# A hybrid encoder trunk on one core: the inverse root's division placed beside ScalarE's root, first rows scaled out of PSUM, two gates moved to VectorE, and a layer norm cut into token tiles

## The chip, the cores and the metric

The kernel runs on one core of one Trainium2 chip. The metric is the device time of one execution in microseconds (us); the median of three runs stands for a kernel.

## The reference

The input `x` has 256 tokens of 2048 features (float32). Two layers follow each other; each is a token mixer and a squared-ReLU MLP (2048 to 8192 to 2048), each with an RMS norm ahead of it and a residual add behind it, and a last RMS norm closes the trunk. The first layer's mixer is the one that the change touches:

```python
def conv_module(h, w_pw1, b_pw1, w_dw, b_dw, ln_g, ln_b, w_pw2, b_pw2):
    u = h @ w_pw1 + b_pw1
    a, gate = jnp.split(u, 2, axis=-1)
    u = a * jax.nn.sigmoid(gate)
    u = lax.conv_general_dilated(...) + b_dw   # causal, depthwise, 31 taps
    u = jax.nn.silu(layer_norm(u, ln_g, ln_b))
    return u @ w_pw2 + b_pw2
```

Here `h` is `x * rsqrt(mean(x*x) + 1e-6) * g`. The second layer's mixer is latent attention, which the change leaves alone but for the inverse roots of its norms.

## The kernel before, in words

All matrix products are made of two float32r parts of each operand, an upper part (`hi`, a copy by ScalarE in `upper_half`, L163) and a lower part (`lo`, the rest, subtracted by VectorE or GpSimd in `lower_half`, L167), in three products. Weights come in pieces of 0.5 to 1 MB on SyncE's queue into three buffers (`load`, L146 to L155). Inside `tc.manual_schedule()` every engine takes its instructions in the order of the program text, so the text is the schedule. TensorE has filler in that schedule: transposes of the identity that nobody reads (`busy` L748, L796, `keep_warm` L233), with counts in `N_WARM`, `N_WARM_GAP` and `N_WARM_LN`.

**The start (L510 to L833).** ScalarE's queue issues the 16 KB of norm gains (`stage_rows`, L514) and then the second 128 tokens of `x`; SyncE's queue issues the first 128 tokens, each in three pieces (L515 to L518). The gains are transposed (L735) and copied to `vecs` (L736). TensorE transposes `x` into PSUM (`turn0`, L762), 8 blocks of 128 columns for each token tile, then 4 more. VectorE takes the mean squares of the first token tile with `bn_stats` (L746), ScalarE those of the second with `Square` (L744). L776 to L784 bring them to `r0`, the inverse root (`rsqrt`, L213 to L226: ScalarE's `Sqrt` L218, then four dependent VectorE steps L222 to L225). TensorE spreads `r0` into a row of PSUM (L787), VectorE copies the row to SBUF (L791), and then scales the transposed blocks in place by gain and row (`scaled`, L798 to L803), block 0 first. ScalarE makes their upper parts (`upper`, L814), VectorE the lower ones (`lower`, L817), and the first products of the convolution's first matrix follow (`conv_mm`, L556 to L569).

**The chunks (L866 to L910).** The 16 chunks of 128 features go by in turn: products of chunk c on TensorE, while chunk c-1 gets its gate (`glu`, L580: a sigmoid on ScalarE, then either one VectorE operation, L588, or a bias on ScalarE, L593, and a product on GpSimd, L594) and its 31 taps. Of the taps, ScalarE starts two sums in PSUM (`start_sum`, L624), VectorE adds most of them (`add_tap`, L653, in an order found by `dve_taps`, L676), ScalarE makes some products apart (`product`, L599) and GpSimd adds those up (`side_sum`, L646). For the last chunk, 15 taps are products with diagonal matrices on TensorE (`last_products`, L617), 7 are added by VectorE, and 8 products are summed by GpSimd.

**The layer norm (L911 to L998).** Each chunk is transposed to tokens (`to_tokens`, L708) for its statistics (`ln_stats`, L719 to L723; the last pair of chunks together by `bn_stats`, L723). `bn_aggr` (L919) gives mean and variance, TensorE spreads them (L926), VectorE subtracts the mean and multiplies by the inverse root (`ln_op`, L930 to L933), ScalarE applies `Silu` (L947), VectorE makes the lower part (L957), and the products of the second matrix follow (L993). Ahead of each new function on ScalarE, `warm` (L228) issues a dummy activation, so that the table is loaded there.

**The end (L1543 to L1582).** `finish` has its own copy of the inverse root (L1556 to L1561), scales the rows and stores them.

## Time and profile before

| what | value |
|---|---|
| median of 3 runs | 1976.75 us (1976.64 to 1977.14) |
| the profiled execution, its own time | 1976.61 us |
| the span of its trace | 1974.8 us |
| TensorE busy | 1959.7 us, 99% |
| VectorE, ScalarE, GpSimd busy | 1265.8, 989.0, 221.4 us |
| moved by DMA | 367.58 MB, mean 186 GB/s |

Times in the rows of a profile are microseconds from the span's start; a timeline row has start, duration (or the stretch that merged instructions fill), engine, line, operation, output and input, count, and in brackets how long the engine had been idle before it and what ended that. PE is TensorE's products, PEld its loads of the stationary operand, DVE is VectorE, ACT ScalarE, POOL GpSimd, SPq and ACTq the queues that issue DMAs. The filler transposes count as busy time of PE, and the ends of products are modelled, so the 99% alone doesn't say that the products set the time.

### The profile page before, as it was taken

The page shows a single profiled execution, that of the slowest core. Times are in us where ns is not written, and L with a number is a line of the kernel's source. Part 1 is how long each engine was busy: PE and PEld are TensorE (multiplying, and loading weights), DVE is VectorE, ACT ScalarE, POOL GpSimd, SP SyncE. Part 2 cuts the span into 40 slices and gives each one's busy share as a digit, 9 for nine tenths or more (in the row PEclk, how much of TensorE's full clock was granted, in tenths as well). Part 3 has the DMA queues.
Part 4 walks back from the last instruction along what each step waited for, and adds up shares of the span by engine and source line. Part 5 has one row for each costly group of instructions (what it writes and reads, how often), then busy time and mean ns, then how long its engine had stood idle before and what let it go on. Part 6 is the DMA issues. An engine that isn't in the chain of part 4 may idle for free.

```text
span 1974.8 us, 27819 instructions
## 1 busy us (share of the span) xinstructions
PE 1959.7 (99%) x10981; PEld 1718.3 (87%) x10981; DVE 1265.8 (64%) x1914; ACT 989.0 (50%) x1427; POOL 221.4 (11%) x183
## 2 busy tenths in 40 slices
PE   9999999999999999999999999999999999999998
PEld 8999888888888888888899998888888888888886
DVE  7999987755444556666656666866555445665554
ACT  5667755544333445444456655554443334544443
POOL 6999100000000000000002310000000000000000
PEclk9999999999999999999999999999999999999999
DMA  7766456665555666556554445666655566665553
GB/s 232 208 187 181 168 182 205 189 190 190 193 196 194 190 188 191 191 191 194 186 186 140 139 150 171 209 196 192 192 192 192 192 191 192 192 192 192 192 192 107
DMA packets 243875, 367.58 MB, mean 186 GB/s; under 512 B 15512, under 2 KB 90528, under 8 KB 243488
## 3 DMA queue, kind: packets, MB, share of 16 engines
q1 hardware_dynamic: 242416, 363.28, 57.9%
q10 hardware_dynamic: 1328, 2.52, 0.4%
q8 instruction: 86, 1.41, 0.3%
q14 instruction: 45, 0.37, 0.0%
HBM read 363.68 MB, written 2.10 MB: 185 GB/s over the span
## 4 chain that ended last, share of the span: by engine, by line
PE 97%; ACT 1%; DVE 1%; DMA 0%; POOL 0%; issue 0%; ACTq 0%; DVEq 0%
PE acc L465 23%; PE acc L198 15%; PE acc L196 15%; PE acc L197 15%; PE acc L466 12%; PE acc L566 9%; PE acc L993 2%; DMA xs<-in_x 0%; PE acc L1380 0%; PE tr L254 0%; ACT hi L163 0%; PE acc L1244 0%; PE acc L1246 0%; PE acc L1245 0%; DVE lo L167 0%; PE tr L1371 0%
## 5 line engine op out<-in xcount | busy, mean ns | idle before, releaser
L167 DVE TENSOR_TENSOR lo<-raw,hi 128x1024 fp32r<-128x1024 f32 (+1 forms) x631 | 760.6, 1211 | 635.3 <-ACT hi L163 630.1
L163 ACT ACTIVATE hi<-raw 128x1024 fp32r<-128x1024 f32 (+1 forms) x696 | 723.3, 1047 | 756.2 <-PE acc L197 427.5
L465 PE MATMUL acc<-xt,hi 128*128 128x512 f32 x2048 | 710.3, 390 | 0.0
L466 PE MATMUL acc<-xt,lo 128*128 128x256 f32 x2048 | 577.5, 282 | 0.0
L465 PEld LDWEIGHTS acc<-xt,hi 128*128 128x128 f32 x2048 | 384.4, 188 | 80.7
L197 PE MATMUL acc<-hi,gl 128*128 128x512 f32 (+1 forms) x1028 | 399.1, 388 | 0.0
L198 PE MATMUL acc<-lo,gh 128*128 128x512 f32 (+1 forms) x1028 | 399.1, 388 | 0.0
L196 PE MATMUL acc<-hi,gh 128*128 128x512 f32 (+1 forms) x1028 | 399.1, 388 | 0.0
L466 PEld LDWEIGHTS acc<-xt,lo 128*128 128x128 f32 x2048 | 387.1, 189 | 0.2
L198 PEld LDWEIGHTS acc<-lo,gh 128*128 128x128 f32 x1028 | 193.0, 188 | 39.8
L197 PEld LDWEIGHTS acc<-hi,gl 128*128 128x128 f32 x1028 | 193.0, 188 | 39.7
L196 PEld LDWEIGHTS acc<-hi,gh 128*128 128x128 f32 x1028 | 193.0, 188 | 39.7
L566 PE MATMUL acc<-xt,hi 128*128 128x256 f32 x1024 | 180.0, 281 | 0.3 <-ACT xt L814 0.2
L653 DVE SCALAR_TENSOR_TENSOR sum<-ub,w_dw,sum 128x256 f32<-128x256 f32 x410 | 164.8, 486 | 4.2 <-ACT sum L624 3.8
L167 POOL TENSOR_TENSOR lo<-raw,hi 128x1024 fp32r<-128x1024 f32 x65 | 155.0, 2409 | 14.8 <-ACT hi L163 14.8
L566 PEld LDWEIGHTS acc<-xt,hi 128*128 128x128 f32 x1024 | 154.6, 188 | 1.1 <-ACT xt L814 0.7
L566 PE MATMUL acc<-xt,lo 128*128 128x256 f32 x512 | 139.2, 279 | 0.0
L566 PEld LDWEIGHTS acc<-xt,lo 128*128 128x128 f32 x512 | 94.6, 188 | 0.0
L1175 POOL MEMSET pad_kv<- 128x8 f32 x1 | 0.1, 105 | 770.7 <-DVE xt L209 770.7
L477 ACT ACTIVATE v<-acc 128x256 f32<-128x256 f32 x128 | 46.3, 382 | 24.9 <-PE acc L466 24.9
L196 PE MATMUL acc<-hi,oh 128*128 128x512 f32 x128 | 50.6, 395 | 0.0
L198 PE MATMUL acc<-lo,oh 128*128 128x512 f32 x128 | 50.0, 391 | 0.0
(272 smaller groups left out, 1724.3 us busy)
## 6 DMA issues: line engine op xcount, KB each, us to landing
raw<-in_mlp_w SPq DMA_DIRECT2D x256, 1024.0 KB, 5.1
raw<-in_conv_w_pw SPq DMA_DIRECT2D x62, 512.0 KB, 5.1
raw<-in_conv_w_pw SPq DMA_DIRECT2D x16, 1024.0 KB, 5.0
raw<-in_mla_w_o SPq DMA_DIRECT2D x16, 1024.0 KB, 5.6
raw<-in_mla_w_kv_up SPq DMA_DIRECT2D x8, 1024.0 KB, 5.6
raw<-in_mla_w_in SPq DMA_DIRECT2D x8, 576.0 KB, 3.7
raw<-in_mla_w_in SPq DMA_DIRECT2D x4, 1024.0 KB
raw<-in_mla_w_q_up SPq DMA_DIRECT2D x16, 256.0 KB, 3.1
```

The lines of the kernel that those rows point to most:

```text
L163: nc.scalar.activation(hi, raw[:, js, :], AF.Copy)
L167: eng.tensor_tensor(lo, raw, hi.bitcast(F32), op=ALU.subtract)
L196: nc.tensor.matmul(ps, sh, mh, start=start, stop=False)
L197: nc.tensor.matmul(ps, sl, mh, start=False, stop=False)
L198: nc.tensor.matmul(ps, sh, ml, start=False, stop=stop)
L465: nc.tensor.matmul(ps[b], wh[:, bs], xhl(k), start=k == 0, stop=False)
L466: nc.tensor.matmul(ps[b][:, :S], wl[:, bs], xh(k), start=False, stop=k == KC - 1)
L477: nc.scalar.activation(v[:, b, :], o[:, S:], AF.Copy)
L566: nc.tensor.matmul(pss[c][b][:, :S], w[i][:, bs], (xh, xl)[j](k), start=k == i + j == 0, stop=end and k == k0 + nk - 1 and (i, j) == terms ...
L653: nc.vector.scalar_tensor_tensor(out=out, in0=ubs[c][:, w : w + S], scalar=tap(c, w), in1=base, op0=ALU.mult, op1=ALU.add)
L993: nc.tensor.matmul(ps2[b][t], x_kt(k, t), w[:, bs], start=k == g == i == 0, stop=k == KC - 1 and i == len(group) - 1,)
L1175: nc.gpsimd.memset(pad_kv, 0.0)
```

## The change

1. **Inverse root.** `rsqrt` and `finish` share `refined`: with `s` the root and `v` the mean square, it divides 1 by `v` (not by `s`), multiplies by `s`, and makes the same Newton step from there. The division needs no root. It is four VectorE operations as before.
2. **Start.** The gains' 16 KB are issued behind `x` on ScalarE's queue; their transposition and copy move from the head of TensorE's and VectorE's order to behind all of `x`'s transpositions; VectorE's copy now stands ahead of L776. Two new VectorE copies (`early`) bring blocks 0 and 1 to SBUF ahead of the last `bn_stats`; `scaled` for these two reads them and takes the spread row straight from PSUM. The row's copy to SBUF goes to ScalarE, behind the first `hi`. The dummy sigmoid moves from there to the end of the first chunk, and half a weight split (the second half of piece 3) moves behind the first gate.
3. **Gates.** The zero margins of the three gate buffers are set once, at the start, on GpSimd. Chunk 14's gate is one VectorE operation, as that of chunks 0 and 15 was.
4. **Last chunk.** Two more taps of chunk 14 go first on VectorE; the last sum of chunk 15 (L882) is cut in two token tiles; the last two chunks have their statistics taken apart (four `bn_stats` of 128 columns, not two of 256) from three PSUM tiles, not one.
5. **Layer norm.** Multiplication by the inverse root and the first `Silu` of block 0 go by token tiles, and the first products take token tile 0 first.
6. **Filler and room.** 6 for 12 transposes ahead of the first products, 1, 9, 4, 6 for 3, 12, 6, 9 around the layer norm; `PAD_SMALL` 48 for 16, and the gate buffers lie in another pool, so that tiles behind them in SBUF lie elsewhere.

```diff
-PAD_SMALL = 16
+PAD_SMALL = 48
-N_WARM = (5, 0, 16, 12)
+N_WARM = (5, 0, 16, 6)
-N_WARM_LN = (3, 12, 6, 9)
+N_WARM_LN = (1, 9, 4, 6)
...
+    def refined(s, v, y, t):
+        nc.vector.reciprocal(t, v)
+        nc.vector.tensor_tensor(y, s, t, op=ALU.mult)
+        nc.vector.scalar_tensor_tensor(out=t, in0=y, scalar=-0.5, in1=s, op0=ALU.mult, op1=ALU.mult)
+        nc.vector.scalar_tensor_tensor(out=y, in0=t, scalar=1.5, in1=y, op0=ALU.add, op1=ALU.mult)
...
-        nc.scalar.activation(t, ms, AF.Sqrt, bias=eps_cols[eps])
+        nc.scalar.activation(r, ms, AF.Sqrt, bias=eps_cols[eps])
         nc.vector.tensor_scalar(v, ms, scalar1=eps, scalar2=None, op0=ALU.add)
-        nc.vector.reciprocal(y, t)
-        nc.vector.scalar_tensor_tensor(out=t, in0=y, scalar=-0.5, in1=y, op0=ALU.mult, op1=ALU.mult)
-        nc.vector.tensor_tensor(t, t, v, op=ALU.mult)
-        nc.vector.scalar_tensor_tensor(out=y, in0=t, scalar=1.5, in1=y, op0=ALU.add, op1=ALU.mult)
+        refined(r, v, y, t)
...
-        vecs_rows = stage_rows(cv, vec_rows, nc.scalar)
         for i in range(3):
             for t in range(T):
                 c0, c1 = X_PARTS[t][i]
                 (nc.sync, nc.scalar)[t].dma_start(xs[:, t, c0:c1], x[0, t * P : (t + 1) * P, c0:c1])
+        vecs_rows = stage_rows(cv, vec_rows, nc.scalar)
...
+        branches = [cv.tile([P, PAD + S], F32, name=nm("ub")) for _ in range(3)]
+        for ub in branches:
+            nc.gpsimd.memset(ub[:, 0:PAD], 0.0)
...
-            ub = ubs[c] = cv2.tile([P, PAD + S], F32, tag="ub", name=nm("ub"), bufs=3)
-            (nc.vector if c in (0, KC - 1) else nc.gpsimd).memset(ub[:, 0:PAD], 0.0)
+            ub = ubs[c] = branches[c % 3]
...
-            if c in (0, KC - 1):
+            if c in (0, KC - 2, KC - 1):
...
-            turn(n_vecs, vecs_rows, misc)
-            nc.vector.tensor_copy(vecs[:, :n_vecs], misc[:, :n_vecs])
...
-            for n in range(NNB):
+            def squares(n):
                 nc.vector.bn_stats(xst[:, n, :], xs[:, 0, n * NB : (n + 1) * NB])
+            for n in range(NNB - 1):
+                squares(n)
...
+            early = [xn[:, 0, (i + 1) * S : (i + 2) * S] for i in range(2)]
+            for i in range(2):
+                nc.vector.tensor_copy(early[i], where[i])
+            squares(NNB - 1)
             for t in range(T):
                 turn0(range(8, 12), t)
+            pss[0] = [acc_tile()]
+            turn(n_vecs, vecs_rows, pss[0][0])
+            nc.vector.tensor_copy(vecs[:, :n_vecs], pss[0][0][:, :n_vecs])
             busy(N_WARM[2])
...
-            nc.vector.tensor_copy(r_row, misc[:, :S])
             conv_half(0, 0)
-            warm(AF.Sigmoid)
-            pss[0] = [acc_tile() for _ in range(2)]
+            nc.scalar.activation(r_row, misc[:, :S], AF.Copy)
+            pss[0].append(acc_tile())
...
-                        out=where[k], in0=where[k], scalar=g_mix[0][:, k : k + 1], in1=r_row,
+                        out=where[k], in0=early[k] if k < 2 else where[k], scalar=g_mix[0][:, k : k + 1],
+                        in1=misc[:, :S] if k < 2 else r_row,
...
-                    conv_split(3)
+                    warm(AF.Sigmoid)
+                    conv_half(3, 0)
...
+                    for _ in range(2):
+                        dve_step(KC - 2, 0)
                     dve_taps(KC - 1)
...
-                    nc.vector.tensor_tensor(ca[:, c, :], last_sum[0], halves[c], op=ALU.add)
+                    for t in range(T):
+                        ts = slice(t * P, (t + 1) * P)
+                        nc.vector.tensor_tensor(ca[:, c, ts], last_sum[0][:, ts], halves[c][:, ts], op=ALU.add)
...
-                if c > 1:
+                if c == 1:
+                    conv_half(n + 1, 1)
+                else:
...
             to_tokens(KC - 1)
+            ln_stats(KC - 2)
             ln_stats(KC - 1)
...
-                    swish(sh[:, k, :], k)
+                    for t in range(T if k == 0 else 1):
+                        swish(sh, k, slice(t * P, (t + 1) * P) if k == 0 else slice(0, S))
...
-            ln_op(0, 1, scale, ALU.mult)
+            for t in range(T):
+                ln_op(0, 1, scale, ALU.mult, t)
...
+                        order = [(b, t) for b in range(2) for t in range(T)]
+                        if k == 0:
+                            order.sort(key=lambda r: r[1])
```

More of the change, by code (lines that the diff above doesn't have):

```diff
@@ L721, in ln_stats @@
                 else:
+                    q, p = 2 * t if c < KC - 1 else 0, KC // 2 - 1 + 2 * (c - KC + 2)
                     out = stats[:, t, p : p + 2, :].rearrange("p a b -> p (a b)")
[L723 removed]
+                    nc.vector.bn_stats(out, cts[c][t][:, q * P : (q + 1) * P])
         for n in range(3):
```

65 lines of the change are left out of this document (31 added, 34 removed).

## The prediction

> **What bounds the kernel now.** I read the head of the page, then the chain of waits, then the timeline around each place where the chain leaves TensorE.
>
> ```profile
> span 1974.8 us, 27819 instructions
> ...
> PE 1959.7 (99%) x10981; PEld 1718.3 (87%) x10981; DVE 1265.8 (64%) x1914; ACT 989.0 (50%) x1427; POOL 221.4 (11%) x183
> ...
> PE 97%; ACT 1%; DVE 1%; DMA 0%; POOL 0%; issue 0%; ACTq 0%; DVEq 0%
> ```
>
> ```profile
> 16.13 1.69 PE acc L566 x12
> ...
> 198.86 0.45 DVE ub L588
> ...
> 211.87 44.08 PE acc L993 x192
> ```
>
> TensorE carries 97% of the chain. It leaves TensorE in three stretches that the change touches: up to 16.13 (loads and first norm), from 198.86 to 211.87 (last gate, last taps, layer norm) and the last norm after 1967. Between them, matmuls follow each other without gaps, so what is saved in a stretch moves all that comes later. The three stretches make some 30 us; the change can win or lose only a part of these, unless it alters the pace of the matmuls.
>
> **Start.** The timeline:
>
> ```profile
> 4.42 0.19 DVE L736 COPY vecs<-acc 128x32 f32<-128x32 f32 x1 [3.52 <-PE acc L287]
> 4.66 1.29 DVE L746 BATCH_NORM_STATS2 xst<-xs 128x6 f32<-128x512 f32 x2
> 5.17 1.48 PE L764 MATMUL sum<-ident,xs 128*128 128x128 f32 x6
> ...
> 9.89 1.91 PE L751 MATMUL acc<-ident 128*128 128x128 f32 x16
> ...
> 10.07 0.16 DVE L776 TENSOR_TENSOR xsq<-xsq 128x1 f32<-128x1 f32 x1 [0.57 <-ACT xn L744]
> ...
> 10.82 0.30 ACT L218 ACTIVATE t<-ms,pad_const 128x2 f32<-128x2 f32 x1 [0.38 <-DVE ms L781]
> ...
> 11.15 0.17 DVE L222 RECIPROCAL y<-t 128x2 f32<-128x2 f32 x1 [0.16 <-ACT t L218]
> ...
> 11.74 0.16 DVE L225 SCALAR_TENSOR_TENSOR y<-t,y 128x2 f32<-128x2 f32 x1
> ...
> 12.43 0.42 DVE L791 COPY xn<-acc 128x256 f32<-128x256 f32 x1 [0.53 <-PE acc L787]
> 12.89 0.49 DVE L800 SCALAR_TENSOR_TENSOR tr<-tr,vecs,xn 128x256 f32<-128x256 f32 x1
> ...
> 13.49 0.37 ACT L814 ACTIVATE xt<-tr 128x256 fp32r<-128x256 f32 x1
> ...
> 13.91 1.69 PE L566 MATMUL acc<-xt,hi 128*128 128x256 f32 x8 [0.21 <-ACT xt L814]
> ```
>
> From the root (10.82) to the first product (13.91) pass 3.09 us. *Root:* four dependent small steps start 0.195 apart (11.15 to 11.74 is three). The mean square with its epsilon (`v`) needs no root and starts beside it. After the change `v` starts at 10.82, the division at 11.02, the product with the root at 11.21 (the root is there, since 11.15 could start on it), and the last step at 11.60 instead of 11.74: 0.14 won. *Row:* `scaled` starts where the copy started, 12.43 instead of 12.89: 0.46 won. An operand in PSUM may cost something; L800 reads and writes PSUM now at 0.49, the copy out of PSUM takes 0.42, so I take nothing. ScalarE's new copy (at most 0.6, after its 1.04 us `hi`) lies beside the first `scaled`. The dummy sigmoid ended just as L814 started; it goes to the end of the first chunk, where only the first gate and a weight split of the next chunk's second half stand behind it; without that cover it would cost its load and itself, 1.28 and 0.20 as in L231's rows below. Sum from the root on: 3.09 less 0.60 is 2.49. All that follows up to 16.13 hangs on `scaled` and shifts with it.
>
> *When the root starts* is the open term. VectorE's copy of the gains is now ahead of L776, behind TensorE's last transposition, which in turn waits for 16 KB behind all of `x`. TensorE had its transpositions out at 9.89 (filler starts). One more, some 0.3 to its end, then the copy (0.19): L776 comes at about 10.35, not 10.07. Against that stand the loads:
>
> ```profile
> 2.00:3.00 1.00, 0.00 (x0) 0.00 (x0) 0.00 (x0) 0.32 (x1) 0.00 (x0) 1.00 0.60 189
> 3.00:4.00 1.00, 0.00 (x0) 0.00 (x0) 0.00 (x0) 0.99 (x2) 0.00 (x0) 1.00 0.92 357
> ...
> raw<-in_conv_w_pw SPq DMA_DIRECT2D x4, 256.0 KB, 8.0
> ```
>
> Until 3 us the DMA engines move 189 GB/s, then 357. With the gains out of the way the second half of `x` fills that hole and lands earlier; but the first half, which had the engines to itself, lands later than 4.66, and TensorE, busy from there to 9.89 without a break, starts later by up to 0.5. Together I take the root 0.4 later (11.2). Ends: 0.3 earlier (all of `x` lands sooner and the copy hides) and 1.2 later (the gains land with the first weights, issued at 2.12 and 8.0 underway, so at 10.1 or after; from landing to root 0.3, 0.2 and the 0.75 from 10.07 to 10.82 make 11.4 with the hops, and half a microsecond more for the weights ahead of them). **Start: 0.2 won, between 0.9 won and 0.6 lost.**
>
> **Last chunk and layer norm.**
>
> ```profile
> 189.73 3.62 DVE L653 SCALAR_TENSOR_TENSOR sum<-ub,w_dw,sum 128x256 f32<-128x256 f32 x9 [0.77 <-ACT sum L624]
> ...
> 198.35 0.28 PE L566 MATMUL acc<-xt,lo 128*128 128x256 f32 x1
> ...
> 198.85 0.45 DVE L588 SCALAR_TENSOR_TENSOR ub<-acc,vecs,sg 128x256 f32<-128x256 f32 x1
> ...
> 199.94 6.11 DVE L653 SCALAR_TENSOR_TENSOR sum<-ub,w_dw,sum 128x256 f32<-128x256 f32 x15 [0.24 <-ACT sum L624]
> 200.82 5.31 POOL L646 TENSOR_TENSOR tp<-tp,tp 128x256 f32<-128x256 f32 x7 [1.05 <-ACT tp L599]
> ...
> 206.50 0.42 DVE L881 TENSOR_TENSOR half<-sum,tp 128x256 f32<-128x256 f32 x1
> ...
> 207.01 0.43 DVE L882 TENSOR_TENSOR ca<-sum,half 128x256 f32<-128x256 f32 x1
> ...
> 207.97 0.76 DVE L723 BATCH_NORM_STATS2 stats<-acc 128x6 f32<-128x256 f32 x2 [0.53 <-PE acc L708]
> 208.65 0.47 DVE L919 BATCH_NORM_AGGREGATE mv<-stats 128x2 f32<-128x27 f32 x2
> ...
> 209.15 0.30 ACT L218 ACTIVATE t<-mv,pad_const 128x2 f32<-128x2 f32 x1 [2.42 <-DVE mv L919]
> ...
> 209.46 1.28 ACT L231 ACT_TABLE_LOAD   x1
> ...
> 210.75 1.21 DVE L933 TENSOR_TENSOR ca<-ca,tr 128x256 f32<-128x256 f32 x3 [0.19 <-PE tr L926]
> 210.76 0.20 ACT L231 ACTIVATE warm<-ident 128x1 f32<-128x1 f32 x1
> 211.21 0.60 ACT L947 ACTIVATE sh<-ca,vecs 128x256 fp32r<-128x256 f32 x1 [0.25 <-DVE ca L933]
> ...
> 212.48 0.43 DVE L957 TENSOR_TENSOR sl__119<-ca,sh 128x256 fp32r<-128x256 f32 x1 [0.52 <-ACT ca L947]
> ...
> 219.26 0.77 PEld L993 LDWEIGHTS acc<-lo,sh 128*128 128x128 f32 x4 [0.27 <-DVE lo L167]
> ```
>
> *Gates.* Chunk 14's gate on VectorE (0.45 as L588) falls into the 0.77 that VectorE sat idle ahead of 189.73, and takes GpSimd and ScalarE out of that path; VectorE's taps come some 0.15 sooner. Chunk 15's gate could start at 198.69 (last product 198.35 plus 0.28 and a hop), not 198.85: 0.15 won, no more, as TensorE sets it.
>
> *Taps.* The two taps moved ahead fill the 0.24 wait for ScalarE's sum. VectorE would then be done 0.5 sooner. But GpSimd's seven additions end at 206.13, and they hang on the gate by way of ScalarE's products: they move by 0.15 only, to 205.98. L881 needs both: 206.03 instead of 206.50, 0.47 won. **GpSimd is late next.**
>
> *Token tiles.* L882's first half, at 206.54, takes about 0.30 (half of 0.43's streaming part saved), its second starts 0.2 behind; the last transposition ends about 207.40, and two of the four short `bn_stats` lie beside it. 256 columns start 0.34 apart, 512 (L746 above) 0.60; so 128 take 0.21. `bn_aggr` comes at 207.81 instead of 208.65: 0.84 won so far, and the root at 208.33.
>
> *Root and first block.* The root's four steps win 0.14 again. The multiplication comes at 209.7 instead of 210.75, in two halves; its first half feeds a half `Silu`, 0.11 shorter. Here ScalarE's table is late next: load and dummy behind the root (209.46 to about 210.96 now) end about 0.8 earlier, at 210.1, and `Silu` starts there, 1.1 before 211.21, and ends 1.2 sooner. But the split doesn't reach the end of the stage: ScalarE's two halves take longer together than one whole, so its second activation, on which L957 waits (212.48), comes 1.0 sooner only. From there VectorE's chain runs to the weight split on which TensorE waits at 219.26, 0.27 today; TensorE will wait some 0.5 there. **Layer norm: 1.0 won**, between 0.5 (GpSimd or the table holds it back) and 1.2 (all of TensorE's lead stays).
>
> By the Trainium skill (page "ScalarE: Activation LUTs", section "What ACT_TABLE_LOAD costs") each switch costs 1.28 us and a drain of 1.38. By that rule `Silu` could not start before 211.3 in the changed kernel, and this stretch would win nothing. The trace agrees on 1.28 (209.46) and not on the drain, since the dummy ran at 210.76.
>
> **End.**
>
> ```profile
> 1967.96 0.21 DVE L1557 TENSOR_SCALAR ms<-ssq,msp 128x1 f32<-128x1 f32 x1 [0.64 <-ACT scratch L381]
> 1968.29 0.16 DVE L1558 RECIPROCAL ys<-ws 128x1 f32<-128x1 f32 x1
> ```
>
> `v` at 1967.96, the division 0.24 later, product 0.2 later at 1968.39; two steps follow it where three followed 1968.29: **0.1 won** (0 to 0.15).
>
> **Sum.** 0.2 + 1.0 + 0.1 = 1.3 us. The profiled execution took 1976.61, 0.14 below the median: 1975.3 on its scale, **1975.4** on that of the median. With all ends at their best 2.25 is won (1974.5), at their worst 0.1 lost (1976.85).
>
> **Filler and room.** Ten filler transposes go from the layer norm, at 0.11 each (16 in 1.91 above) some 1.1 us of filler, and that stretch gets about that much shorter; six go ahead of the first products, where 0.6 is won. So idle gaps should stay near today's. What moves in SBUF behind the pad is a stationary operand at most (the norm's outputs, the MLP's inner values); weights that stream, and `xt`, lie ahead of it or on the other side. I cost this at nothing.
>
> **Rivals.**
> *a. The gains land late* (0.17). For it: their 16 KB stand last in ScalarE's queue, and compete with weights from then on. Root at 12.0, start 0.6 lost: 1976.2. Against: only two small packets per engine.
> *b. `x` lands sooner and the copy hides* (0.12). The hole before 3 us speaks for it; root at 10.5, start 0.9 won: 1974.7. Against: TensorE's unbroken row up to 9.89.
> *c. The norm's win stops at GpSimd or the table* (0.08), 0.5 or less of it left: 1976.0.
> *d. TensorE's clock falls* (0.05); this one is slower. Six transposes took 1.48 us at 5.17, sixteen 1.91 at 9.89: a start at 0.21, then 0.11 each, so half speed until about 8.5, four microseconds from TensorE's first work. If the thinner filler lets the clock fall in a stretch, the products behind run at half speed for as long, and 2 us are lost each time; one such fall outweighs the 1.3 (1977.4), and the first stretch, the norm and, where it flickers, one more make 1981. It decides once TensorE's gaps grow well beyond the longest that the norm has today:
>
> ```profile
> PEld acc L708 <- DVE ca L882: 0.6, 1, 0.6
> ```
>
> By the Trainium skill ("TensorE: Matmul & The Clock Gate", section "What's actually happening") activity is weighed in windows of 3.4 us, and a window must be idle: by that it doesn't fall here.
> *e. The moved tiles change the matmuls' pace* (0.03, either sign): 0.3% of TensorE's 1959.7 us is 6, so 1969 or 1981. Against: nothing that streams is moved.
>
> **Chances.** The forecast itself, 1975 to 1975.9, has 0.55. 0.2% is 3.95 us, about what a measurement of this kernel can tell from no change. By the sum no more than 2.25 can be won, so faster than that needs *e* with its good sign: 0.02. Slower needs *d* in several places or *e*: 0.04. Within: 0.94. For 8 in 10 I take 1974.2 to 1977.0, which holds the forecast, *a*, *b* and *c* and leaves *d* and *e* out.
>
> **What would show it.** First product (L566) near 13.7, with the root near 11.2 and 2.5 us between them; if L776 waits long for the gains' copy, *a*. Last gate at 198.7 less the start's win, L881 released by GpSimd, `bn_aggr` 9.1 after the gate's start (9.8 today), the first L993 11.9 after it (13.0 today); a longer wait than 0.27 for the weight split behind. Matmul means of the MLP's groups unchanged; if they move, *e*; if products behind the norm take twice as long, *d*. The sum is wrong if VectorE's order, and not TensorE or GpSimd, turns out to be what the two stretches wait for.

## The result, and the profile after

The changed kernel takes 1979.68 us (median of 22 runs, 1978.75 to 1980.52); the kernel before took 1976.82 in 22 runs beside it (1976.5 to 1977.4). The ratio is 1.0014, with a 95% interval from 1.0008 to 1.0021: 2.9 us slower, where 1.3 faster was forecast. That is less than the 0.2% taken as the bound for "no change", but the time lies 2.7 above the top of the range. The profiled execution took 1979.47.

The page's head, and its shares of the chain of waits:

```profile
span 1977.7 us, 27792 instructions
...
PE 1958.4 (99%) x10965; PEld 1716.5 (87%) x10965; DVE 1266.4 (64%) x1918; ACT 987.5 (50%) x1428; POOL 220.1 (11%) x171
...
PE 96%; DVE 2%; ACT 1%; issue 0%; POOL 0%; DMA 0%; DVEq 0%; ACTq 0%
```

TensorE works 1.3 us less than before (1958.4 for 1959.7) in a span that is 2.9 longer (1977.7 for 1974.8): it waits more, and the question is where. Comparing the start of the same product in the two traces, counted back from the last one, gives the lag at each place:

| place | before | after | lag |
|---|---|---|---|
| first product of the first chunk | 13.91 | 15.89 | +1.98 |
| last gate (chunk 15) | 198.85 | 200.70 | +1.85 |
| first `bn_aggr` | 208.65 | 209.76 | +1.11 |
| first product behind the layer norm | 211.87 | 212.70 | +0.83 |
| a product of the first MLP | 365.70 | 366.93 | +1.23 |
| the 40th product after it | 372.69 | 375.52 | +2.83 |
| root of the last norm | 1967.96 | 1970.82 | +2.86 |

So the start lost 2.0, last chunk and layer norm won 0.75 (1.98 to 1.23), a stretch of the MLP that the prediction never looked at lost 1.6, and the end won nothing.

**Start**, the timeline of the changed kernel (start, stretch, engine, line, operation, then the idle time ahead of it and what ended that):

```profile
6.58 1.29 DVE L753 BATCH_NORM_STATS2 xst<-xs 128x6 f32<-128x512 f32 x2 [5.68 <-DMA xs<-in_x]
...
6.69 0.45 PE L774 MATMUL tr<-ident,xs 128*128 128x128 f32 x1 [6.69 <-DMA xs<-in_x]
...
7.14 1.49 PE L774 MATMUL sum<-ident,xs 128*128 128x128 f32 x6
...
9.95 0.42 DVE L786 COPY xn<-tr 128x256 f32<-128x256 f32 x1 [1.13 <-PE tr L774]
...
10.62 0.68 DVE L753 BATCH_NORM_STATS2 xst<-xs 128x6 f32<-128x512 f32 x1
...
11.84 0.24 PE L287 MATMUL acc<-ident,stage 32*128 32x32 f32 x1
...
12.12 0.19 DVE L792 COPY vecs<-acc 128x32 f32<-128x32 f32 x1 [0.82 <-PE acc L287]
...
12.96 0.29 ACT L223 ACTIVATE r<-ms,pad_const 128x2 f32<-128x2 f32 x1 [2.91 <-DVE ms L799]
...
13.83 0.16 DVE L218 SCALAR_TENSOR_TENSOR y<-t,y 128x2 f32<-128x2 f32 x1
...
14.52 0.38 ACT L811 ACTIVATE xn<-acc 128x256 f32<-128x256 f32 x1 [0.31 <-PE acc L805]
...
14.93 0.49 DVE L818 SCALAR_TENSOR_TENSOR tr<-xn,vecs,acc 128x256 f32<-128x256 f32 x1 [0.94 <-ACT xn L811]
...
15.89 0.90 PE L570 MATMUL acc<-xt,hi 128*128 128x256 f32 x4 [0.76 <-ACT xt L833]
```

The first half of token tile 0 is there at 6.58, not 4.66: the two token tiles are now issued at once and share the DMA engines, where the 16 KB of gains used to hold ScalarE's queue back (its first packet of `x` began at 3.70; now at 2.58) and leave the engines to tile 0. From 3 to 4 us SyncE's queue, with tile 0, had 84.2% of the engines' time and ScalarE's 7.4%; in the changed kernel they have 48.7 and 48.5%. TensorE starts with it (6.69), cold, at half pace (six transpositions in 1.49). VectorE's order follows TensorE: the early copies wait 1.13 for its transpositions, the last statistic (10.62) stands behind them, the gains' copy (12.12) waits 0.82 more, for their transposition, which TensorE has last, and the sum of squares behind that. The root starts at 12.96 for 10.82. The chain of waits shows one thing more, first in the changed kernel, then the same place in the timeline of the kernel before:

```profile
8.63 1.07 PE acc L761 x5
```

```profile
7.72 0.18 PEld L764 LDWEIGHTS tr<-ident,xs 128*128 128x128 f32 x1 [0.41 <-DMA xs<-in_x]
```

Five filler transpositions stand between the two token tiles. Before, TensorE had to wait for tile 1 there anyway; now tile 1 is in SBUF (ScalarE squares it from 6.83), and the filler is 1.07 us of the chain. No run took it out.

From root to first product pass 2.93, not 2.49: the first scaled row waits 0.94, until ScalarE's copy of the row is done.

**Last chunk and layer norm:**

```profile
200.70 0.48 DVE L591 SCALAR_TENSOR_TENSOR ub<-acc,vecs,sg 128x256 f32<-128x256 f32 x1
...
208.03 0.42 DVE L903 TENSOR_TENSOR half<-sum,tp 128x256 f32<-128x256 f32 x1
...
209.76 0.49 DVE L946 BATCH_NORM_AGGREGATE mv<-stats 128x2 f32<-128x33 f32 x2
...
210.28 0.30 ACT L223 ACTIVATE r<-mv,pad_const 128x2 f32<-128x2 f32 x1 [1.69 <-DVE mv L946]
...
210.60 1.28 ACT L231 ACT_TABLE_LOAD   x1
...
211.89 0.20 ACT L231 ACTIVATE warm<-ident 128x1 f32<-128x1 f32 x1
...
212.16 0.88 ACT L975 ACTIVATE sh<-ca,vecs 128x128 fp32r<-128x128 f32 x2
...
212.70 0.50 PE L1027 MATMUL acc<-hi,sh 128*128 128x512 f32 x1 [0.25 <-ACT sh L975]
...
213.71 0.43 DVE L988 TENSOR_TENSOR sl__119<-ca,sh 128x256 fp32r<-128x256 f32 x1 [0.60 <-ACT ca L975]
...
220.47 0.76 PEld L1027 LDWEIGHTS acc<-lo,sh 128*128 128x128 f32 x4 [0.45 <-DVE lo L167]
```

From the last gate to `bn_aggr` pass 9.06 us (9.80 before), to the first product 12.00 (13.02). The lag goes from 1.85 to 0.83; then 0.4 of it comes back, because L988 (lag 1.23) and the weight split behind it gain less, and TensorE waits 0.45 for that split, not 0.27.

**First MLP.** Five rows of the changed kernel's timeline:

```profile
349.90 0.40 ACTq L1060 DMA_DIRECT2D v<-in_positions  x1
...
356.35 0.17 DVE L1062 CAST v<-v 128x2 f32<-128x2 int32 x1 [3.68 <-DMA v<-in_positions]
...
356.43 1.23 DVE L167 TENSOR_TENSOR lo<-raw,hi 128x1024 fp32r<-128x1024 f32 x1
...
370.78 1.08 DVE L478 TENSOR_TENSOR v<-acc,v 128x256 f32<-128x256 f32 x3
...
371.25 0.50 PE L465 MATMUL acc<-xt,hi 128*128 128x512 f32 x1 [1.39 <-DVE v L478]
```

and the same stretch of the kernel before:

```profile
348.68 0.39 ACTq L1026 DMA_DIRECT2D v<-in_positions  x1
...
353.51 0.17 DVE L1028 CAST v<-v 128x2 f32<-128x2 int32 x1 [2.07 <-DMA v<-in_positions]
...
353.60 1.23 DVE L167 TENSOR_TENSOR lo<-raw,hi 128x1024 fp32r<-128x1024 f32 x1
...
367.94 1.08 DVE L478 TENSOR_TENSOR v<-acc,v 128x256 f32<-128x256 f32 x3
```

`rotary_tables` loads the token positions (256 packets of 4 bytes) on ScalarE's queue while the MLP runs, and VectorE casts them, in order, ahead of the next weight split. The load lasts 6.45 us from issue to cast, where it lasted 4.83; each thing behind it on VectorE is 2.8 later (356.43 for 353.60, 370.78 for 367.94), and L478, which empties TensorE's accumulators, is then too late. In the trace of DMA packets, a fetch of TensorE's instructions (16 KB, 0.88 us, queue 8) begins at 354.08, in the midst of the position load's packets (353.65 to 355.46); before, the nearest fetch began at 347.15 and the packets took 352.20 to 353.19.

**End:**

```profile
1970.82 0.30 ACT L1590 ACTIVATE ws<-ssq,msp 128x1 f32<-128x1 f32 x1
...
1971.92 1.12 ACT L1603 ACTIVATE xs<-xs,ys 128x256 f32<-128x256 f32 x2 [0.80 <-DVE ys L218]
```

From root to scaling 1.10 us; before, 1.11 (root 1967.96, scaling 1969.07).

### The profile page after: what moved, and what is told of

The parts are those of the page before. It is cut to its first block, busy times and chain, and to the rows that moved or that the text cites. A ratio compares the mean times of both kernels' runs of the same rounds, so it can differ in the third digit from the quotient of the medians.

```text
span 1977.7 us, 27792 instructions
## 1 busy us (share of the span) xinstructions
PE 1958.4 (99%) x10965; PEld 1716.5 (87%) x10965; DVE 1266.4 (64%) x1918; ACT 987.5 (50%) x1428; POOL 220.1 (11%) x171
## 3 DMA queue, kind: packets, MB, share of 16 engines
q8 instruction: 86, 1.41, 0.3%
## 4 chain that ended last, share of the span: by engine, by line
PE 96%; DVE 2%; ACT 1%; issue 0%; POOL 0%; DMA 0%; DVEq 0%; ACTq 0%
PE acc L465 23%; PE acc L198 15%; PE acc L196 15%; PE acc L197 15%; PE acc L466 12%; PE acc L570 8%; PE acc L1027 2%; DVE sum L656 1%; PE acc L1414 0%; PE tr L254 0%; ACT hi L163 0%; DMA xs<-in_x 0%; PE acc L1278 0%; PE acc L1279 0%; PE acc L1280 0%
## 5 line engine op out<-in xcount | busy, mean ns | idle before, releaser
L465 PE MATMUL acc<-xt,hi 128*128 128x512 f32 x2048 | 710.4, 390 | 1.4 <-DVE v L478 1.4
L465 PEld LDWEIGHTS acc<-xt,hi 128*128 128x128 f32 x2048 | 384.4, 188 | 82.4 <-DVE v L478 1.7
L198 PE MATMUL acc<-lo,gh 128*128 128x512 f32 (+1 forms) x1028 | 399.1, 388 | 0.0
L196 PE MATMUL acc<-hi,gh 128*128 128x512 f32 (+1 forms) x1028 | 399.1, 388 | 0.0
L198 PEld LDWEIGHTS acc<-lo,gh 128*128 128x128 f32 x1028 | 193.0, 188 | 40.1
L196 PEld LDWEIGHTS acc<-hi,gh 128*128 128x128 f32 x1028 | 193.0, 188 | 39.4
L196 PE MATMUL acc<-hi,oh 128*128 128x512 f32 x128 | 50.6, 395 | 0.0
L198 PE MATMUL acc<-lo,oh 128*128 128x512 f32 x128 | 50.0, 391 | 0.0
```

What stands on the lines that cost most here:

```text
L196: nc.tensor.matmul(ps, sh, mh, start=start, stop=False)
L198: nc.tensor.matmul(ps, sh, ml, start=False, stop=stop)
L465: nc.tensor.matmul(ps[b], wh[:, bs], xhl(k), start=k == 0, stop=False)
```

## Experiments

The theory after the result: (1) the gains behind `x` cost the start 2 us, because tile 0 lands later and VectorE's statistics now hang on TensorE; (2) the layer norm part works as forecast; (3) the filler counts move a fetch of TensorE's instructions onto the position load. Rivals: the early copies or the row's copy alone are to blame for the start; the fillers cost through the clock; the MLP stall comes from the moved tiles. The kernel before took 1976.8 to 1977.0 beside each group of runs.

### The two halves of the loss, undone one at a time

**Gains first** (a1): the changed kernel with its gains issued ahead of `x` again.

```diff
+        vecs_rows = stage_rows(cv, vec_rows, nc.scalar)
         for i in range(3):
             ...
-        vecs_rows = stage_rows(cv, vec_rows, nc.scalar)
```

> The changed kernel with one thing undone: the 16 KB of gains are issued ahead of x again. Theory A (the order of the loads): with the gains ahead, the second half of x starts late and the first half has the DMA engines to itself, lands near 4.7 instead of 6.6, and TensorE's transpositions, which start with it and run at half speed, end 2 us sooner; the root starts near 11.0 instead of 12.96, and the start gets 1.9 us shorter. Rival: VectorE's copy of the gains, which stands ahead of the statistics, holds the root back; then the root stays near 12.9, as that copy is still there. On the wait of 1.66 us in the MLP at 369.6: if it comes from the count of TensorE's instructions, which is unchanged here, it stays (1.6 us at 367.7), and the kernel takes about 1977.6; if it comes from when that stage starts, it may go, and the kernel takes about 1976.0.

**Old fillers** (a2): the changed kernel with the old counts.

```diff
-N_WARM = (5, 0, 16, 6)
+N_WARM = (5, 0, 16, 12)
-N_WARM_LN = (1, 9, 4, 6)
+N_WARM_LN = (3, 12, 6, 9)
```

> The changed kernel with the old counts of filler transposes (5, 0, 16, 12 and 3, 12, 6, 9), 16 more than it has. Theory B: the load of the positions in the MLP lands 1.6 us later than before because a piece of TensorE's instructions is fetched over the same DMA engines just then, and where that fetch falls depends on how many instructions TensorE has had; with the 16 back, the wait of 1.39 us of L465 for L478 near 370 goes and the kernel takes about 1978.0. Rival: the wait comes from the tiles that were moved or from the shifted start; then it stays, and the kernel takes 1979.6. The start stays 2 us longer under both.

**New fillers alone** (b1): the kernel before with the new counts, the reverse of that diff, and nothing else.

> The kernel before with the new counts of filler transposes alone (6 for 12 ahead of the first products, 1, 9, 4, 6 for 3, 12, 6, 9). Theory B: the fetch moves as in the changed kernel, the load of the positions lands 1.6 us later and L465 waits some 1.4 us near 368: 1978.4. Rival: the fillers are only filler; 1976.8, and no wait there. If the thinner filler let TensorE's clock fall (my rival d), the products after 211 would take twice as long for a while, 2 us more.

**Row to a scratch tile** (a3): gains first, and ScalarE's copy of the row goes to a tile that nothing else uses there.

```diff
-            r_row = xn[:, 0, 0:S]
+            r_row = scratch[:, :S]
```

> As a1_gains_first, and the spread row is copied by ScalarE to another tile in SBUF (scratch) instead of the tile that also holds the two early blocks. In the changed kernel the first scaled block waits 0.94 us, until that copy ends (14.90), though it reads the row from PSUM. If it waits because both lie in one SBUF tile, the wait goes and the first product comes 0.4 us sooner than in a1_gains_first. If it waits because two engines read one PSUM bank, it stays, and the two kernels take the same time.

| run | median us (range) | ratio, 95% | first product | longest step near 369 |
|---|---|---|---|---|
| a1 | 1977.7 (1976.91 to 1978.81) | 1.0003 [0.9993, 1.0013] | 14.26 | 1.26 |
| a2 | 1978.68 (1977.8 to 1979.02) | 1.0008 [0.9999, 1.0017] | 16.88 | as elsewhere |
| b1 | 1978.19 (1977.96 to 1978.56) | 1.0005 [0.9996, 1.0015] | 14.50 | 1.36 |
| a3 | 1977.7 (1976.83 to 1978.48) | 1.0004 [0.9995, 1.0013] | 14.94 | 1.26 |

The last column is the longest time from one product's start to the next; it is 1.67 in the changed kernel and 0.12 or 0.23 elsewhere in that stretch. The four intervals all hold 1, so what follows rests on the rows of one trace each, and the medians only agree with it.

Timeline of a1:

```profile
4.52 1.29 DVE L753 BATCH_NORM_STATS2 xst<-xs 128x6 f32<-128x512 f32 x2 [3.62 <-DMA xs<-in_x]
...
10.48 0.19 DVE L792 COPY vecs<-acc 128x32 f32<-128x32 f32 x1 [0.55 <-PE acc L287]
...
11.33 0.30 ACT L223 ACTIVATE r<-ms,pad_const 128x2 f32<-128x2 f32 x1 [0.40 <-DVE ms L799]
...
13.30 0.49 DVE L818 SCALAR_TENSOR_TENSOR tr<-xn,vecs,acc 128x256 f32<-128x256 f32 x1 [0.94 <-ACT xn L811]
```

With the gains first, tile 0 lands at 4.52 again, the root comes at 11.33 and 2.0 us of time come back, 1.63 of them at the first product: the issue order is most of the start's loss. The root still waits for the gains' copy (0.55 behind TensorE). In a3, whose trace has TensorE at full clock from 10.24 (a1: from 7.44), the root came at 12.00 with tile 0 equally early: the root follows TensorE's clock. a3 also leaves the first scaled row's wait at 0.94, so it isn't the tile that the copy writes; the two engines share only the PSUM bank that both read. b1 has the MLP gap without any moved tile, a2 has the moved tiles without the gap: the filler counts decide, and the moved tiles don't. a2 missed its time by 0.7: the gap went as expected, but in its trace full clock came at 12.37 (10.52 in the changed kernel) and the first product 1.0 later.

### The positions loaded early

**First try** (c1 to c4): positions and frequencies go to two new tiles in the `const` pool, loaded in the convolution on SyncE's queue; c1 is the changed kernel with that alone.

```diff
+        pos_i = const.tile([P, T], I32, name="pos_i")
+        fr = const.tile([P, DR // 2], F32, name="fr")
...
                     nc.sync.dma_start(b2, conv_b_pw2[0:1, :].partition_broadcast(P))
+                    nc.sync.dma_start(pos_i, positions[0].rearrange("(t p) -> p t", p=P))
+                    nc.sync.dma_start(fr, inv_freq[0:1, :].partition_broadcast(P))
```

> The changed kernel, with the positions and the rotary frequencies loaded during the convolution, on SyncE's queue behind the bias of the second projection, instead of beside the first MLP products on ScalarE's queue. Theory: the MLP stall of the change (1.66 us at 369.6) is the late landing of the position packets behind TensorE's instruction fetch, so it vanishes whatever the filler counts: 1979.7 - 1.6 = about 1978.1, no gap over 1 us near 369, and the layer norm stage 0.7 us shorter than before as in the changed kernel. Rival: the fetch delays VectorE's weight split through something else (the weights' own load, or the split itself), and the gap stays: 1979.7.

c2 takes the start of the kernel before (gains first, statistics free of TensorE, row copied by VectorE, old filler counts there):

> The start of the kernel before (gain rows behind... as before: ahead of x, statistics not tied to TensorE, row copied on VectorE, old filler counts there), the refined root of the change, the layer norm part of the change with its filler counts, and the early load of positions. Theory: what the change does in the layer norm is worth 0.74 us by itself and the MLP stall is gone with the early load: 1976.8 - 0.7 = about 1976.1, the first product where the kernel before has it (13.9, with about 0.05 less from the root). Rival: the layer norm's gain is eaten by a longer wait at the weight split (0.08 us there in the changed kernel's trace, 0.3 or more without the late start): 1976.8.

c3 has gains first and `nc.scalar.activation(r_row, ...)` behind `scaled(0, 1)`:

> The changed kernel with the gain rows ahead of x, the positions loaded early, and ScalarE's copy of the row put behind the first two scaled rows instead of ahead of them. Theory: the first scaled row waits for ScalarE's copy because both read one PSUM bank (0.94 us of wait in the run with gains first, of which the copy itself is about 0.4); with the copy behind, the first product comes 2.5 us after the root instead of 2.93. Time: 1977.7 (gains first) - 1.26 (its MLP stall) - 0.4 = about 1976.0 at the same clock phase. Rival: the wait is for the spread of the row by TensorE, and the order of the two readers is worth nothing: 2.9 us from root to first product, 1976.4.

c4 has gains first and the three copies of VectorE behind `r0 = rsqrt(...)`:

> The changed kernel with the gain rows ahead of x, the positions loaded early, and VectorE's two early copies and its copy of the gain rows put behind the inverse root instead of ahead of the statistics, so that no statistic waits for TensorE. Theory: the root of the change is late because these copies wait for transpositions at a cold clock; without them the root starts at about 10.8 whatever the clock's phase (gains first: 11.33, with a row copy to scratch 12.0), and the spread between executions at the start is smaller. Time: 1977.7 - 1.26 - 0.5 = about 1975.9 to 1976.2. Rival: the root waits for the statistics themselves or for ScalarE's squares and stays at 11.3: 1976.4; or the copies then stand ahead of the scaled rows and give it back: 1976.4.

All four missed by 11 to 14 us: 1989.49, 1989.89, 1989.8, 1989.65 (ratios 1.0063 or 1.0064, each at least 1.0049). There was no gap near 369, so the stall was gone, yet the whole kernel ran slower. The groups of TensorE's products, of the kernel before and of c1:

```profile
L465 PE MATMUL acc<-xt,hi 128*128 128x512 f32 x2048 | 710.3, 390 | 0.0
L466 PE MATMUL acc<-xt,lo 128*128 128x256 f32 x2048 | 577.5, 282 | 0.0
```

```profile
L465 PE MATMUL acc<-xt,hi 128*128 128x512 f32 x2048 | 719.2, 393 | 0.0
L466 PE MATMUL acc<-xt,lo 128*128 128x256 f32 x2048 | 579.2, 283 | 0.0
```

The products in which `xt` is the streaming operand are some 0.3 to 0.8% longer (these two, and the convolution's with 283 ns for 281); the MLP's second products (L196 to L198), in which weights stream, take 388 ns in both. The lag grows steadily from the convolution to the end (3.0 us at the first product, 4.7 behind the layer norm, 14 at the end). The two tiles hold 136 bytes of each partition, ahead of almost all others. That suspicion was the next run.

**The same load into room that was there** (d1): the padding tile holds positions and frequencies; no other tile moves.

```diff
-        pos_i = const.tile([P, T], I32, name="pos_i")
-        fr = const.tile([P, DR // 2], F32, name="fr")
+        pos_i = pad_right[:, 0:T].bitcast(I32)
+        fr = pad_right[:, T : T + DR // 2]
```

> The changed kernel with the positions and frequencies loaded early, as in the first try of that (1989.5), but kept in the padding tile that the kernel has already, so that no other tile moves in SBUF. In the first try the products of line 465 took 393 ns each for 390 and the whole kernel ran 0.5% slower with no gap on TensorE; two tiles of 136 bytes had been put ahead of nearly everything. Theory: that was the shift of the other tiles, and the MLP stall is the late landing of the positions; now the means go back to 390 ns, the gap near 369 is gone, and the time is 1979.7 - 1.6 = about 1978.1. Rival: the early load itself disturbs the convolution's loads on SyncE's queue; the time stays near 1989.

The same in the kernel before with the new filler counts (d4):

> The kernel before with the new filler counts and the early positions in its padding tile, nothing else. With the new filler counts alone it took 1978.2 (1.4 more than before), with a gap of 1.36 on TensorE at 368.9. Theory: the fillers cost only by moving TensorE's instruction fetch onto the position load, so with the load early they cost nothing: 1976.8, no gap near 369. Rival: fewer fillers cost by themselves (a clock that falls, a later start): 1978.2.

d1 took 1977.83 (1977.31 to 1979.18; ratio 1.0005 [0.9997, 1.0014]), d4 1976.98 (1976.55 to 1977.95; ratio 1.0 [0.9991, 1.0009]); both came within 0.3 of what was expected, the means are 390 again and no gap is left near 369. So the early load is worth 1.85 in the changed kernel and 1.2 in the other; fewer fillers cost nothing by themselves here; and 136 bytes of shift alone made c1 11.7 us slower than d1.

### Still fewer fillers

The link by way of the instruction fetch was so far only read from traces. Taking away 16 more fillers should put the fetch 16 products later against the load: if the fetch is the link, the stall must go; if fewer fillers cost by themselves, it must stay or grow.

```diff
-N_WARM = (5, 0, 16, 6)
+N_WARM = (5, 0, 4, 2)
```

In the changed kernel (e1):

> The changed kernel with 16 filler transposes fewer still in its start (counts 5, 0, 4, 2 for 5, 0, 16, 6), positions loaded where the change loads them. Theory: a fetch of TensorE's instructions (16 KB, one for each 128 products with their loads, some 0.3 us apart there) comes 16 pairs, 4.7 us, later against the position load than in the changed kernel, where it fell 0.4 us behind the first position packet; so it falls behind the last one, the packets take 1.0 us again, the cast of the positions waits about 2.1 and not 3.7, and the gap near 369 is gone: 1979.7 - 1.6 = about 1978.1, plus up to 1 if the products start at half clock. Rival: fewer fillers lengthen the wait by themselves, whatever the fetch does: the gap stays at 1.4 or grows, 1979.7 or more.

and in the kernel before with the new layer norm counts (e2):

> The kernel before with the change's filler counts in the layer norm and 16 fewer than the change in the start (5, 0, 4, 2). With the change's own counts it took 1978.2 and had the gap of 1.36. Theory: the fetch comes some 4.7 us later, behind the position packets; no gap near 369, positions wait about 2.1: 1976.8, plus up to 1 if the products start at half clock. Rival: fewer fillers make the gap; it stays or grows: 1978.2 or more.

Timeline of e1, then of e2:

```profile
355.83 0.17 DVE L1062 CAST v<-v 128x2 f32<-128x2 int32 x1 [2.04 <-DMA v<-in_positions]
```

```profile
355.52 0.17 DVE L1028 CAST v<-v 128x2 f32<-128x2 int32 x1 [2.08 <-DMA v<-in_positions]
```

The stall is gone in both; no gap is left near 369. e1 took 1978.6 (1978.27 to 1979.21; ratio 1.0008 [0.9999, 1.0018]), e2 1977.82 (1976.59 to 1978.48; 1.0004 [0.9995, 1.0014]). The packets of eight traces (the positions' and those of the frequencies, loaded behind them), by where the fetch began against them, and how many products TensorE had started by then:

| kernel | packets of the load | fetch begins | products started | wait of the cast |
|---|---|---|---|---|
| before | 352.20 to 353.19 | 347.15 | 2374 | 2.07 |
| a2 | 354.51 to 355.48 | 349.38 | 2374 | 2.06 |
| a1 | 351.87 to 353.50 | 352.28 | 2390 | 3.29 |
| a3 | 352.59 to 354.32 | 352.72 | 2389 | 3.29 |
| after | 353.65 to 355.46 | 354.08 | 2391 | 3.68 |
| b1 | 352.87 to 354.84 | 352.85 | 2388 | 3.38 |
| e2 | 354.24 to 355.21 | 355.07 | 2376 | 2.08 |
| e1 | 354.66 to 355.51 | 355.39 | 2376 | 2.04 |

The load's packets take 0.85 to 1.0 us where the fetch comes well ahead of them or in their last quarter, and 1.6 to 2.0 where it falls on their first half. How it holds them up is seen by counting packets of queue 10 in the changed kernel from 353.6 to 354.7 and from 355.0 to 355.6 (one more lies between), and in the kernel before from 352.1 to 353.3 (queue, packets, MB, share):

```profile
q10 hardware_dynamic: 390, 0.02, 22.3%
```

```profile
q10 hardware_dynamic: 25, 0.00, 5.7%
```

```profile
q10 hardware_dynamic: 416, 0.02, 21.7%
```

390 of the 416 packets are through at once; the last 26 come when the fetch (354.08, 0.88 long) has ended. 26 is a sixteenth of 416, as many as one of the 16 DMA engines has if they are dealt out evenly: the one that carries the fetch, it seems (the trace doesn't name engines). In a1 and b1, too, 26 packets come last, at the end of the fetch (353.21) or 0.8 behind it (353.77). So the stall went as expected, and in the eight traces it is there when the fetch falls on the first half of the load, whatever the number of fillers. The expected distance did not come: the fetch came 0.3 and 0.85 later against the first packet, not 4.7. That this was enough for its engine's share to be through was luck. Two parts of the estimate fail in the traces: products start there 0.17 apart, not 0.3 (130 in the 22.18 us ahead of the changed kernel's fetch), and the fetch doesn't come at a fixed count of products (2374, 2388 to 2391, 2376). What sets that count stays open, so the number of fillers alone doesn't tell where a fetch will fall.

What e1 and e2 lost elsewhere is TensorE's clock. Granted clock by stretch (columns: stretch, its length, busy time and count of PE, PEld, DVE, ACT, POOL, granted clock, DMA share, GB/s), of e1:

```profile
17.10:20.40 3.30, 3.30 (x16) 3.30 (x17) 3.23 (x8) 2.62 (x6) 3.21 (x2) 0.50 0.51 154
20.50:24.00 3.50, 3.50 (x33) 3.50 (x32) 3.46 (x8) 3.34 (x6) 3.50 (x2) 1.00 0.89 260
```

After a gap of 1.2 ahead of its first product the clock fell for 3.41 us (17.02 to 20.44 in the clock's records; e2: 16.27 to 19.69, also 3.41), and e1 came to the layer norm's first product at 213.85 for 212.70. This is the prediction's rival *d*, provoked: one fall costs some 1.2 us. The Trainium skill ("TensorE: Matmul & The Clock Gate", section "What's actually happening") says that activity is weighed in windows of 3.4 us; the length of both falls agrees. That a window must be idle, as the prediction has it, does not: in the 3.41 us ahead of each fall TensorE was busy for 1.78 us (e1) and 2.06 (e2). With 2.40, in e1's window before that, and 2.53, in the changed kernel's at the same place, the clock held.

### The parts that work

**Layer norm part alone** (d2): c2 with the positions in the padding tile.

> As the earlier run of the layer norm part alone (start of the kernel before, refined root, layer norm of the change, early positions), with the positions in the padding tile. Theory: 1976.8 - 0.7 = about 1976.1, no MLP stall, the four waits at the layer norm as in the changed kernel. Rival: the win of the layer norm is only there because the start is late (a longer time in which GpSimd and the loads run ahead), and with the early start the norm wins nothing: 1976.8.

**Both repaired** (d3): gains first, VectorE's copies behind the root, row copy behind the first upper half, positions in the padding tile.

```diff
             scaled(0, 1)
             upper(g[0])
+            nc.scalar.activation(r_row, misc[:, :S], AF.Copy)
```

> The changed kernel with the gain rows ahead of x, VectorE's three copies behind the inverse root (statistics free of TensorE), ScalarE's row copy behind the first upper half, and the early positions in the padding tile. With the row copy right behind the two scaled rows the first product came 3.25 us after the root, since the copy waited for the second scaled row and held the first upper half up; now the first upper half starts about 0.13 after the first scaled row and the product comes about 2.5 us after the root. Theory: root at 10.8 to 11.4 as x lands, first product about 13.6, layer norm 0.7 won, no MLP stall: about 1975.8. Rival: the later rows wait for the copied row and the second product gap takes the gain back: 1976.2.

d2 took 1976.03 (1975.73 to 1976.5; ratio 0.9996 [0.9987, 1.0005]), d3 1975.92 (1975.6 to 1976.62; 0.9994 [0.9985, 1.0003]), before beside them 1977.01: both lower by about 1.0, though the intervals don't exclude none. In d2 the lag against the kernel before goes from +0.37 at the first product (14.28) to -0.40 behind the layer norm: 0.77 won, with an early start as with the late one. d3's start wins nothing against the kernel before (first product 13.90 for 13.91; 13.6 was expected), so its gain, too, is the layer norm's. The row copy's place is seen by c3, where it stood ahead of the first upper half, and d3:

```profile
14.06 0.38 ACT L848 ACTIVATE xn<-acc 128x256 f32<-128x256 f32 x1 [1.21 <-DVE acc L819]
...
14.34 0.38 ACT L834 ACTIVATE xt<-tr 128x256 fp32r<-128x256 f32 x1
```

```profile
11.25 0.30 ACT L223 ACTIVATE r<-ms,pad_const 128x2 f32<-128x2 f32 x1 [0.38 <-DVE ms L798]
...
12.96 0.48 DVE L819 SCALAR_TENSOR_TENSOR tr<-xn,vecs,acc 128x256 f32<-128x256 f32 x1
...
13.47 0.38 ACT L834 ACTIVATE xt<-tr 128x256 fp32r<-128x256 f32 x1 [0.98 <-DVE tr L819]
...
13.90 1.81 PE L572 MATMUL acc<-xt,hi 128*128 128x256 f32 x8 [0.49 <-ACT xt L834]
```

In c3 the copy waited for the second scaled row, which reads the same bank, and held the upper half up: 3.25 us from the root (11.52) to the first product (14.77), a miss against 2.5. In d3 the copy stands one place further back and the way takes 2.65. c4, with the copies of VectorE behind the root, left the root at 11.36: there it waited 0.75 for ScalarE's squares and not for TensorE. So freeing the statistics brought the root no further than about 11.3 in these runs, with tile 1 of `x` as the next limit.

## Why the prediction was wrong, point by point

**Start: the step that failed.** The prediction had the root "0.4 later (11.2)"; it came 2.14 later (12.96). It saw that "the first half, which had the engines to itself, lands later than 4.66", and priced that with TensorE's later start at "up to 0.5": the first half came 1.9 later, and TensorE's start 2.0. It expected the second half of `x` to fill the hole before 3 us (189 GB/s); the changed kernel moves 180 there, so the second half came at the first one's cost. Its row of TensorE, "busy from there to 9.89 without a break", hides five fillers and a wait for tile 1; the fillers are now on the chain. The tie of the statistics to TensorE by the gains' copy was priced, at 0.28; a1, a3 and c4 show that it is worth 0 to 0.65 by itself, by the phase of TensorE's clock, once tile 0 is early. The early copies ahead of the last statistic, which it didn't weigh, cost nothing here: that statistic is done at 11.30, and the gains' copy comes at 12.12. Rival *a* (root at 12.0, "the gains land late") had the sign and half of the size, by another cause: the last packet of the gains was in at 9.26, and TensorE came to them at 11.84. Not the gains were late, but `x`.

*Root:* 0.14 was forecast for four steps of which the first two no longer wait for the root. Measured from root to last step: 0.87 for 0.92 at the start, 0.90 for 0.91 at the end. The product with the root waits for both division and root and starts 0.27 or 0.28 behind the division (0.195 between other steps), so about 0.05 is won at the start and 0.01 at the end. The 0.1 of the end is not there.

*Row:* 0.46 was forecast for scaling out of PSUM. The copy was still in the way, since it and the scaled rows read one bank: 2.93 from root to product for 3.09. d3, with the copy behind, has 2.65. The Trainium skill ("PSUM — Partial Sum Buffer", section "PSUM bank collisions raise a hardware error") says that the compiler orders two engines' accesses to one bank, reads among them; the waits of 0.94 in the changed kernel and in a3 agree. That rule speaks against this step, and the prediction did not weigh it.

**Last chunk and layer norm: right in mechanism, 0.75 for 1.0 in size.** The gate won 0.13 (forecast 0.15), L903 0.45 (0.47), `bn_aggr` 0.87 (0.84), the multiplication 0.89 (1.05), the first `Silu` 1.03 (1.1), the first product 1.15 (1.2); each of these is the lag of 1.98 less that at the place. Then ScalarE's second activation, forecast 1.0 sooner for L957, gave 0.75, and that is what remains behind the weight split, where TensorE waits 0.45 (forecast 0.5). GpSimd was late next, as said: its last addition, done at 208.00, releases L903 (208.03). The table load was not: the dummy was over at 212.09, and `Silu` (212.16) followed the first half of the multiplication (211.84, 0.30), by 0.05. (One gate moved to VectorE, that of chunk 14; the title's two is a slip.) The drain behind the table load that the prediction cites doesn't show here either: the dummy started 0.01 behind the 1.28 of the load. d2 gives the same 0.77 from another start, so rival *c* falls.

**Filler costed at nothing: wrong by 1.6.** The clock was watched, and it held; the cost came by a path that was not on the list, TensorE's own instructions. With the change's counts a 16 KB fetch falls on a load of tiny packets that VectorE waits for in order, some 140 us behind the last filler; with the old counts, and with still fewer, it doesn't.

**Moved tiles costed at nothing: right** (L465's mean is 390 in both), but c1 shows how near that was: 136 bytes more cost 11.7 us, about twice the price of rival *e*.

**Rival *d*** did not happen in the changed kernel. e1 and e2 show one such fall each, and its price is 1.2, not 2.

**Sum.** Forecast -1.3; measured +1.98 (start), -0.75 (layer norm), +1.60 (MLP), +0.03 (end), together +2.86 in the profiled executions and in the medians alike. With start and load repaired (d3) it is -1.1 by the medians and -0.8 by the profiled executions. That comes near the forecast partly by luck: the start, priced at 0.2, and the end, priced at 0.1, win nothing.

## What to carry to other kernels

Where loads are reordered, ask which queue was kept waiting by the transfer that moves: here 16 KB at the head of one queue kept half of `x` off the DMA engines, so that the half needed first came 2 us earlier. A small load that an engine waits for in order can be held up by transfers that the program doesn't issue: loaded early, into room that existed, it cost nothing and took 1.2 to 1.9 us out. And where instructions are added or taken away at one place, compare the waits of the whole trace, not only of the edited stretch: the lag of the same product, counted from the end, shows in one table where the time went.

## What the hardware showed that was not expected

- TensorE's instructions arrive in fetches of 16 KB, one for about 128 products with their loads. The page of the changed kernel has, for all of it:

```profile
q8 instruction: 86, 1.41, 0.3%
```

  They cost TensorE nothing, but hold up small packets: 26 of 416 waited for 0.9 us. The Trainium skill ("Runtime: NRT & Kernel Launch", section "Instruction fetch mechanics") has blocks of 16 KiB or 256 instructions on a DMA queue of their own; the trace agrees (1.41 MB in 86, for 21930 products and loads). It calls the cost mostly hidden, which is so for TensorE and wasn't for VectorE.
- The clock's first rise had no fixed place: full clock came at 8.52 in the kernel before and at 10.25 in b1, which has the same program up to there; at 7.44 in a1 and 12.86 in e2. Both falls lasted 3.41 us, and neither needed an idle window.
- The place of tiles in SBUF can set the pace of the products: 136 bytes ahead of nearly all tiles took L465 from 390 to 393 ns, and the kernel from 1977.83 to 1989.49. Only the products in which `xt` streams slowed; which address does it was not tried.
